# The down phase of a feed-forward block: residual tiles that stay on chip, and outputs transposed per half of the frames

## The chip, the cores and the metric

One core of a Trainium2 chip runs the whole program: one launch for one streaming step of a one-layer encoder trunk. The metric is the device time of one execution in microseconds (us), taken as the median of repeated runs. The core has five engines that take part here: TensorE (PE in the profile, with its weight loads as PEld), VectorE (DVE), ScalarE (ACT), GpSimd (POOL) and SyncE (SP). Sixteen DMA engines move data between the chip's memory (DRAM) and the on-chip tiles; SP, ACT and POOL each issue DMAs into a queue of their own, which the profile numbers q1 (SP), q10 (ACT) and q0 (POOL).

## The reference

Only the last lines of the layer matter to the change. `x` is the residual after attention and convolution; 512 prompt frames and 64 sample frames go through the same weights.

```python
    x = x + mix @ w_out
    h2 = rmsnorm(x, g_norm2)
    x = x + (jax.nn.silu(h2 @ w_gate) * (h2 @ w_up)) @ w_down
    return x, k, v, new_conv
```

Everything is float32. The model width D is 2048 (16 tiles of 128 rows, KD = 16) and the feed-forward width is 5632, which is 22 pairs of 128-row tiles (NFP = 22). The two outputs that come from the last `x` are `y_prompt` (512 x 2048) and `y_sample` (64 x 2048), with frames as rows.

## The kernel before

**Layout.** The 576 frames stand side by side (512 prompt, then 64 sample) and are cut into two halves of 288 columns (HALF, HALVES). Activations lie transposed: channels on the 128 partitions, frames along the free axis. A float32 product is made of three matmuls on a rounded part and a remainder: a weight or activation is split into a high part (a cast to fp32r) and a low part (the difference), and w_hi x_hi, w_lo x_hi and w_hi x_lo are added up in PSUM. `split` (L217 the cast on ScalarE, L218 the subtraction on VectorE) does this for weights and for activations.

**Units and products.** The feed-forward block is computed by Strassen-Winograd on 2 x 2 blocks: two output tiles of 128 channels by two halves of the frames, in seven products numbered `p_` = 1 to 7 instead of eight. One such piece of work is a unit. There are 42 gate and up units (NGU = 42) and then 36 down units, listed in `DOWN` as (d, a, b): output pair d (of eight), over the hidden pairs a to b. A down unit with m = b - a pairs has 7 products of m steps of 3 matmuls, 21m in all. The 36 units together go over each of the 8 x 22 combinations once; the last unit of each of the eight d's is among the last eight units (numbers 28 to 35 of the phase, with m = 7, 3, 7, 7, 3, 7, 5, 6), and `last` holds them.

**The order of the work.** PE's instructions run in the order in which the program gives them (the list `order`: mostly products 1, 3 and 4 of one unit interleaved with those of the next); a scheduler of the framework places those of the other engines. In `run`, products 1, 6, 5 and 3 accumulate in one PSUM tile `psy`, of which ScalarE copies out a `part` after 1, 6 and 5 (`kept`, L1076) before PE may go on adding to it; products 7 and 4 use `psw`, product 2 uses `psx`. After products 2, 5, 3 and 4 `done` hands over one block of the 2 x 2: (0,0), (1,1), (0,1) and (1,0), where the first number is the channel tile c and the second the half i.

**Weights of a down unit.** SP issues them (`load_weight`, L180), two loads per unit, into two buffers each, one unit ahead. `prepare` forms the sums and differences on VectorE (L1052 to L1056) and splits the operand of a product two products ahead (AHEAD = 2).

**The slots.** The hidden activations, in the seven forms that the products need and already split, are written to DRAM by the gate and up units (`put_form`, L923, on POOL's queue) and come back per hidden pair into one of seven tiles, the slots: 128 x 7 x 2 x 288 floats, 2016 KB each. `load_pair` (L1157 to L1160) does it with ScalarE's queue. Slots 0 to 2 take the room of the phase before, the operands h2ah, h2al and b22 of the gate and up units in `h2pool`; slots 3 to 6 lie in `dpool`, which is opened when the down phase begins. Twenty-two pairs go through seven slots, so slots are loaded again as soon as the last unit that uses them is through: `calls` lists after which unit.

**The residual.** It is `x2`, which the out projection left in DRAM (`x2_dram`), as the room on chip is taken by the gate and up units. `load_x2` (L1131 whole, L1140 in halves, POOL's queue) brings the two tiles of a unit's d, two units ahead. `add` (L1154, VectorE) adds the PSUM blocks and parts of a unit to them. `store_x2` (L1146 whole, L1150 in halves, POOL's queue) writes them back to DRAM after the unit, so that the next unit of the same d reads them again; a last unit calls `store_y` instead.

**The outputs.** `store_y` turns blocks of the finished residual on PE into PSUM (L1174; L1179 for the 64 sample frames), in groups of 1, 2 or 3 blocks of 128 frames as they become complete, copies a group into the tile `ob` (two buffers, VectorE, L1175) and stores it from POOL's queue (L1176). The sample frames go through `obs` (ScalarE, L1181) and ScalarE's queue (L1182). The work is placed by `pipe`, a list of generators that is run as the matmul steps go by; `yield 3` lets three steps pass.

Of the kernel before, what the change touches and what calls it, by code (L numbers as in the profile page):

```python
# [10 lines left out]
F32 = mybir.dt.float32  # L11
F32R = mybir.dt.float32r
# [81 lines left out]
def tile_hybrid_stream_step(  # L94
# [739 lines left out]
    h2ah = h2pool.tile([P, KD, HALF], F32R, tag="h2ah", name="h2ah")  # L834
    h2al = h2pool.tile([P, KD, HALF], F32R, tag="h2al", name="h2al")
    b22 = h2pool.tile([P, 2, NP, HALF], F32R, tag="b22", name="b22")
    b22h, b22l = b22[:, 0], b22[:, 1]
# [5 lines left out]
    def h2(kt, i):  # L843
        if i == 0:
            return h2ah[:, kt, :], h2al[:, kt, :]
        hi, lo = (b22h, b22l) if kt % 2 else (b12h, b12l)
        return hi[:, kt // 2, :], lo[:, kt // 2, :]
# [156 lines left out]
    def frames(n, p_):  # L1004

        kind, _, a, m = UNITS[n]
        if kind == "down":
            return [(slots[a + j][:, p_ - 1, 0, :], slots[a + j][:, p_ - 1, 1, :]) for j in range(m)]
        if p_ < 3:
            return [(h2ah[:, k, :], h2al[:, k, :]) for k in range(p_ - 1, KD, 2)]  # L1010
        if p_ == 3:
            return [(b22h[:, j, :], b22l[:, j, :]) for j in range(m)]
        q = {5: 0, 6: 1, 7: 2, 4: 3}[p_]
        return [(tsum[j][:, 0, q, :], tsum[j][:, 1, q, :]) for j in range(m)]
# [55 lines left out]
    def run(n, p_):  # L1070
# [8 lines left out]
        def done(c, i, ps, part=None):  # L1079
            if kind != "down":  # L1080
                return finish(kind, fp, c, i, ps, part)
            add(n, c, i, ps)
            if part is not None:
                add(n, c, i, part)
            if n in last:
                store_y(n, c, i)
            elif (c, i) == (1, 0):
                store_x2(n)
# [34 lines left out]
    first_last = min(last)  # L1123
    spare = [(tmp, "y"), (tmp, "r")], [(tmp, "sq"), (h2pool, "hx")]

    def load_x2(n):

        d, xb = UNITS[n][1], {}
        if n % 4 < 2 or n >= first_last:
            whole = down["pool"].tile([P, 2, T], F32, tag="x2", name=f"x2_{n}", bufs=2)  # L1130
            nc.gpsimd.dma_start(out=whole, in_=x2_dram[2 * d : 2 * d + 2].rearrange("k p t -> p k t"))  # L1131
            xb["whole"] = whole
        for c in range(2):
            for i, (a, b) in enumerate(HALVES):
                if "whole" in xb:
                    xb[c, i] = whole[:, c, a:b]
                    continue
                pool, tag = spare[n % 2][c]
                xb[c, i] = pool.tile([P, HALF], F32, tag=tag, name=f"x2_{n}", bufs=2)
                nc.gpsimd.dma_start(out=xb[c, i], in_=x2_dram[2 * d + c][:, a:b])  # L1140
        xt2[n] = xb

    def store_x2(n):
        d, xb = UNITS[n][1], xt2.pop(n)
        if "whole" in xb:
            nc.gpsimd.dma_start(out=x2_dram[2 * d : 2 * d + 2].rearrange("k p t -> p k t"), in_=xb["whole"])  # L1146
            return
        for c, i in ((0, 0), (1, 1), (0, 1), (1, 0)):
            a, b = HALVES[i]
            nc.gpsimd.dma_start(out=x2_dram[2 * d + c][:, a:b], in_=xb[c, i])  # L1150

    def add(n, c, i, src):
        dst = xt2[n][c, i]
        nc.vector.tensor_tensor(out=dst, in0=src, in1=dst, op=ALU.add)  # L1154

    def load_pair(p):
        tag = ("h2ah", "h2al", "b22", "s3", "s4", "s5", "s6")[p % SLOTS]  # L1157
        pool = h2pool if p % SLOTS < 3 else down["pool"]
        slots[p] = pool.tile([P, FORMS, 2, HALF], F32R, tag=tag, name=f"slot{p}")
        nc.scalar.dma_start(out=slots[p].bitcast(F32), in_=hid_dram[p])  # L1160

    def store_y(n, c, i):

        x2t, cs = xt2[n]["whole"][:, c, :], slice((2 * UNITS[n][1] + c) * P, (2 * UNITS[n][1] + c + 1) * P)
        whole = (c, 1 - i) in unit[n].setdefault("done", set())
        unit[n]["done"].add((c, i))
        b0, b1 = ((0, 2), (3, 4), (0, 3), (2, 4))[2 * whole + i]

        def work():
            yield 3  # L1170
            ob = down["pool"].tile([P, 3, P], F32, tag="ob", name="ob", bufs=2)[:, : b1 - b0]
            po = misc("pot")[:, : (b1 - b0) * P]
            for q in range(b0, b1):
                nc.tensor.transpose(po[:, (q - b0) * P : (q - b0 + 1) * P], x2t[:, q * P : (q + 1) * P], ident)  # L1174
            nc.vector.tensor_copy(out=ob, in_=po.rearrange("p (i c) -> p i c", c=P))  # L1175
            nc.gpsimd.dma_start(out=yp[b0 * P : b1 * P, cs].rearrange("(i p) c -> p i c", p=P), in_=ob)  # L1176
            if i:
                po2 = misc("pot2")
                nc.tensor.transpose(po2[:TS, :P], x2t[:, TP:], ident)  # L1179
                os_ = down["pool"].tile([TS, P], F32, tag="obs", name="obs", bufs=2)  # L1180
                nc.scalar.copy(out=os_, in_=po2[:TS, :P])  # L1181
                nc.scalar.dma_start(out=ys[:, cs], in_=os_)  # L1182
# [6 lines left out]
    for k_, (n, p_) in enumerate(order):  # L1189
# [4 lines left out]
        if (n, p_) == (NGU, 1):  # L1194
# [3 lines left out]
            load_x2(n)  # L1198
            load_pair(3)
            load_x2(n + 1)  # L1200
# [5 lines left out]
        if n == NGU - 1:  # L1206
            for p in {2: (0, 1), 3: (2,)}.get(p_, ()):
                load_pair(p)
        if n >= NGU and p_ == 4:
            if n + 2 < NU:  # L1210
                load_x2(n + 2)
# [37 lines left out]
```

## Time and profile before

| | us |
|---|---|
| runs shown | 2516.25, 2513.17, 2509.73 |
| median | 2513.17 |
| profiled execution, its own time | 2509.96 |
| span of that execution in the profile | 2508.2 |
| PE busy in the span | 2429.6 |
| VectorE / ScalarE / POOL busy | 1756.1 / 1069.1 / 311.5 |
| DMA moved in the span | 369.53 MB |
| of that from 1920 us on (the down phase) | 131.04 MB |

The span goes from the first to the last instruction that the profile shows; the execution's own time has 1.8 us more around it. The mean granted TensorE clock was 0.988. In the down phase, the stretch from 1920 us to the end, the DMA engines' time is shared by queues as follows (packets, megabytes, share of the sixteen engines' time in that stretch):

```profile
q1 hardware_dynamic: 88742, 44.87, 27.1%
q0 software_dynamic: 12576, 43.72, 22.1%
q10 hardware_dynamic: 4160, 41.81, 18.4%
```

The queue q1 carries the weights, q10 the slots (and the small sample outputs), q0 what POOL issues: the residual in both directions, the last forms and the prompt outputs. The transfers of the residual and the slots in the same stretch, with the number of issues, the kilobytes of each and the median us from issue to landing:

```profile
slot<-hid_dram ACTq DMA_DIRECT2D x20, 2016.0 KB, 11.1
...
x<-x_dram POOLq DMA_DIRECT2D x22, 576.0 KB, 4.5
...
x<-x_dram POOLq DMA_DIRECT2D x56, 144.0 KB, 4.8
x_dram<-x POOLq DMA_DIRECT2D x56, 144.0 KB, 5.2
x_dram<-x POOLq DMA_DIRECT2D x14, 576.0 KB, 3.3
```

And the instructions that use the residual and the output tile there (line, engine, operation, names, shapes, count, busy us and mean ns of one, then the idle time just before them and what ended it):

```profile
L1154 DVE TENSOR_TENSOR x<-part,x 128x288 f32<-128x288 f32 x108 | 49.2, 455 | 14.7 <-ACT part L1076 13.4
...
L1175 DVE COPY ob<-pot 128x256 f32<-128x256 f32 (+2 forms) x32 | 13.3, 421 | 6.9 <-PE pot L1174 5.3 <-DMA out_dram<-ob 1.4
```

Rows of this kind give the duration of one instruction and say how long its engine stood before it; a wait counts against the end only where PE, which carries most of the chain, stands too.

### The profile page before, as it was taken

The numbers are of one execution on the slowest core, as the hardware profiler recorded it, in microseconds if no ns is written. First come the engines' busy times: TensorE is split into PE (matmuls) and PEld (weight loads), VectorE is DVE, ScalarE is ACT, GpSimd is POOL, SyncE is SP. The second block draws the span as 40 slices with busy tenths as digits, with TensorE's granted clock in tenths as the row PEclk, the third lists the DMA queues.
The fourth block names the chain that finished last, engine by engine and source line by source line (L and its number), as shares of the span: only waits on it lengthen the run. The fifth ranks groups of instructions, "written<-read, shape, count | busy, mean of one in ns | idle before, by whom it ended". The sixth has DMA issues, their size and how long they took to land.

```text
span 2508.2 us, 44014 instructions
## 1 busy us (share of the span) xinstructions
PE 2429.6 (97%) x18121; PEld 2415.6 (96%) x18121; DVE 1756.1 (70%) x2772; ACT 1069.1 (43%) x1863; POOL 311.5 (12%) x545
## 2 busy tenths in 40 slices
PE   8999999999999999999999999999997898999898
PEld 8999999999999999999999999999997898999898
DVE  7766666353345458888888888888885776777676
ACT  6655555231122345444444444444442343433343
POOL 2111011110020120000010100100001221111121
PEclk9999999999999999999999999999999898999999
DMA  8322332222242343445444444445446767768753
GB/s 265 88 85 86 90 93 79 70 83 85 85 160 85 104 141 101 134 148 153 133 139 131 152 150 140 141 122 157 144 144 237 258 201 270 264 204 274 250 151 97
DMA packets 442690, 369.53 MB, mean 147 GB/s; under 512 B 11198, under 2 KB 413240, under 8 KB 439672
## 3 DMA queue, kind: packets, MB, share of 16 engines
q1 hardware_dynamic: 413624, 233.39, 32.1%
q0 software_dynamic: 24416, 87.38, 9.6%
q10 hardware_dynamic: 4448, 45.94, 4.7%
q8 instruction: 142, 2.33, 0.4%
q14 instruction: 60, 0.49, 0.1%
HBM read 285.85 MB, written 80.82 MB: 146 GB/s over the span
## 4 chain that ended last, share of the span: by engine, by line
PE 90%; DMA 4%; DVE 2%; issue 2%; ACT 1%; POOL 0%; SPq 0%; POOLq 0%; ACTq 0%; DVEq 0%
PE psy L1066 30%; PE pj L209 23%; PE psw L1066 15%; PE pjo L209 8%; PE psx L1066 7%; DMA raw<-in_w_down_dram 3%; PE pw L981 2%; DVE whl L218 1%; DMA hid_dram<-form 1%; PE z L547 1%; PE po L613 1%; DMA slot<-hid_dram 0%; PE os L643 0%; PE zs L573 0%; DVE x L1154 0%
## 5 line engine op out<-in xcount | busy, mean ns | idle before, releaser
L217 ACT CAST whl<-raw 128x1024 fp32r<-128x1024 f32 (+5 forms) x468 | 416.9, 897 | 281.1 <-issue 108.7
L218 DVE TENSOR_TENSOR whl<-raw,whl 128x1024 fp32r<-128x1024 f32 (+5 forms) x468 | 479.5, 1030 | 78.4 <-ACT whl L217 77.5
L209 PE MATMUL pj<-xhi,whi 128*128 128x288 f32 x1504 | 450.6, 300 | 0.6 <-ACT whi L172 0.6
L209 PE MATMUL pj<-xlo,whi 128*128 128x288 f32 x1504 | 444.6, 296 | 1.7 <-DVE xlo L343 1.7
L209 PE MATMUL pj<-xhi,wlo 128*128 128x288 f32 x1504 | 444.3, 295 | 0.3 <-DVE wlo L173 0.3
L1066 PE MATMUL psy<-slot,whl 128*128 128x288 f32 x2112 | 310.5, 303 | 55.2 <-ACT part L1076 19.5
L1066 PEld LDWEIGHTS psy<-slot,whl 128*128 128x128 f32 x2112 | 295.6, 194 | 59.5 <-ACT part L1076 20.3
L209 PEld LDWEIGHTS pj<-xlo,whi 128*128 128x128 f32 x1504 | 284.0, 189 | 2.1 <-DVE xlo L343 2.1
L209 PEld LDWEIGHTS pj<-xhi,whi 128*128 128x128 f32 x1504 | 284.3, 189 | 1.2 <-ACT whi L172 0.8
L209 PEld LDWEIGHTS pj<-xhi,wlo 128*128 128x128 f32 x1504 | 284.4, 189 | 0.9 <-DVE wlo L173 0.5
L1066 PE MATMUL psy<-tsum,whl 128*128 128x288 f32 x2016 | 281.1, 295 | 1.2 <-DVE whl L218 1.2
L1066 PE MATMUL psw<-tsum,whl 128*128 128x288 f32 x2016 | 281.0, 295 | 0.5 <-DVE ut L960 0.5
L1066 PEld LDWEIGHTS psy<-tsum,whl 128*128 128x128 f32 x2016 | 271.8, 189 | 1.5 <-DVE whl L218 1.5
L1066 PEld LDWEIGHTS psw<-tsum,whl 128*128 128x128 f32 x2016 | 271.8, 188 | 0.7 <-DVE ut L960 0.7
L172 ACT CAST whi<-raw 128x1024 fp32r<-128x1024 f32 (+1 forms) x138 | 140.0, 1031 | 232.3 <-PE pj L209 95.8
L1076 ACT COPY part<-psy 128x288 f32<-128x288 f32 x234 | 93.2, 398 | 327.5 <-PE psy L1066 325.6
L923 POOL DMA_DIRECT2D hid_dram<-form x154 | 83.6, 543 | 904.0 <-DVE form L218 759.9
L173 DVE TENSOR_TENSOR wlo<-raw,whi 128x1024 fp32r<-128x1024 f32 (+1 forms) x132 | 160.3, 1227 | 24.5 <-ACT whi L172 23.2
L1066 PE MATMUL psw<-slot,whl 128*128 128x288 f32 x1056 | 155.5, 298 | 0.0
L1066 PEld LDWEIGHTS psw<-slot,whl 128*128 128x128 f32 x1056 | 146.0, 190 | 0.2 <-DVE whl L218 0.2
L1066 PE MATMUL psy<-b,whl 128*128 128x288 f32 x1008 | 140.4, 295 | 0.5 <-ACT part L1076 0.5
L1066 PE MATMUL psx<-h2ah,whl 128*128 128x288 f32 x672 | 135.6, 297 | 2.6 <-DVE gs L960 2.6
(337 smaller groups left out, 4237.2 us busy)
## 6 DMA issues: line engine op xcount, KB each, us to landing
raw<-in_w_in_dram SPq DMA_DIRECT2D x47, 1024.0 KB, 5.4
raw<-in_w_gate_dram SPq DMA_DIRECT2D x44, 1024.0 KB, 5.6
raw<-in_w_up_dram SPq DMA_DIRECT2D x44, 1024.0 KB, 5.9
hid_dram<-form POOLq DMA_DIRECT2D x154, 288.0 KB, 2.5
slot<-hid_dram ACTq DMA_DIRECT2D x22, 2016.0 KB, 11.8
raw<-in_w_down_dram SPq DMA_DIRECT2D x30, 640.0 KB, 5.9
raw<-in_w_out_dram SPq DMA_DIRECT2D x16, 1024.0 KB, 5.2
x<-x_dram POOLq DMA_DIRECT2D x22, 576.0 KB, 4.5
```

Of the source, the lines that this page charges most:

```text
L172: nc.scalar.copy(out=hi[:, a:b], in_=raw[:, a:b])
L173: lo_eng.tensor_tensor(out=lo[:, a:b], in0=raw[:, a:b], in1=hi[:, a:b].bitcast(F32), op=ALU.subtract)
L209: mm(ps, w_[:, k, csl], x_[:, k, a:b], start=(k == 0 and n == 0), stop=(k == nk - 1 and n == 2))
L217: nc.scalar.copy(out=hi, in_=src)
L218: (lo_eng or nc.vector).tensor_tensor(out=lo, in0=src, in1=hi.bitcast(F32), op=ALU.subtract)
L547: mm(zb[i], a_[:, kk], b_[:, q0:TP], start=(n == 0), stop=False, skip_group_check=True)
L613: mm(po[:, i * P : 512], a_[:, i, :], b_[:, : 512 - i * P], stop=(i == 0 and n == 2), **kw)
L923: nc.gpsimd.dma_start(out=hid_dram[fp][:, n - 1], in_=t.bitcast(F32))
L981: mm(pss[j, i], w_[:, k, j * P : (j + 1) * P], x_, start=(kk == 0 and k == 0 and n == 0), stop=(kk == 1 and k == 7 and n == 2))
L1066: mm(ps, whl[:, w_, j, :], x_, start=(start and j == 0 and q == 0), stop=(j == len(xs_) - 1 and q == 2), skip_group_check=True)
L1076: nc.scalar.copy(out=t, in_=st["y"])
```

## The change

In the down phase the residual is loaded once per output pair d and stays on chip until it is turned and stored; `store_x2` is gone. The room for the eight pairs (sixteen tiles of 576 frames) is put together from tiles that the phase has no other use for:

- The operands of the gate and up units in `h2pool` are laid out anew: three tiles of fourteen 288-column pieces (tags s0 to s2, which become slots 0 to 2 later) and one of six (h2z). The operands that product 3 of the gate and up units reads (`late`) fill the third tile and the end of the fourth. h2z later holds the residual of d = 0 and one channel tile of d = 3.
- d = 1 and 2 and the other tile of d = 3 lie in `dpool` (tag x2, ten buffers); d = 4 and 5 in the temporaries y, r, sq and hx; d = 6 in the room of the row scale R; d = 7 in that of the split forms (hl).

All residual loads are now half tiles, four per d, still on POOL's queue, 32 in all. The slot loads move from ScalarE's queue to POOL's (`load_pair`). At the start of the down phase slot 2 and the residual of d = 0 are asked for after product 3 of the last up unit, and the residual of a later d is asked for two units ahead of its first use.

The outputs are turned per half: each block (c, i) is turned as soon as it is done, in two pieces of 128 frames and one of 32, so that a last unit has 12 transposes in place of 10. VectorE copies the two large pieces and ScalarE the small one into `ob`, which has one buffer; the stores are all on POOL's queue: two for half 0, and four for half 1, where the prompt's end (frame 512) cuts a piece in two (`put`).

```diff
--- before.py
+++ after.py
@@ -831,10 +831,14 @@
 
 
     h2pool = tc.alloc_tile_pool(name="h2pool", bufs=1, reuse_waits="tile", side="left")
-    h2ah = h2pool.tile([P, KD, HALF], F32R, tag="h2ah", name="h2ah")
-    h2al = h2pool.tile([P, KD, HALF], F32R, tag="h2al", name="h2al")
-    b22 = h2pool.tile([P, 2, NP, HALF], F32R, tag="b22", name="b22")
-    b22h, b22l = b22[:, 0], b22[:, 1]
+    SB = 2 * FORMS
+    h2t = [h2pool.tile([P, SB, HALF], F32R, tag=f"s{i}", name=f"h2_{i}") for i in range(3)]
+    h2t.append(h2pool.tile([P, 3 * KD - 3 * SB, HALF], F32R, tag="h2z", name="h2_z"))
+    places = [h2t[i][:, j, :] for i in range(3) for j in range(SB)] + [h2t[3][:, j, :] for j in range(3 * KD - 3 * SB)]
+    early, late = places[: 2 * SB] + places[3 * SB : 3 * SB + 4], places[2 * SB : 3 * SB] + places[3 * SB + 4 :]
+    h2a = [(early[2 * k], early[2 * k + 1]) for k in range(KD)]
+    b22s = [(late[2 * j], late[2 * j + 1]) for j in range(NP)]
     b12pool = tc.alloc_tile_pool(name="b12pool", bufs=1, reuse_waits="tile", side="left")
     b12h = b12pool.tile([P, NP, HALF], F32R, name="b12h")
     b12l = b12pool.tile([P, NP, HALF], F32R, name="b12l")
@@ -842,9 +846,8 @@
 
     def h2(kt, i):
         if i == 0:
-            return h2ah[:, kt, :], h2al[:, kt, :]
-        hi, lo = (b22h, b22l) if kt % 2 else (b12h, b12l)
-        return hi[:, kt // 2, :], lo[:, kt // 2, :]
+            return h2a[kt]
+        return b22s[kt // 2] if kt % 2 else (b12h[:, kt // 2, :], b12l[:, kt // 2, :])
 
     def after_b2(kt):
         for i, (a, b) in enumerate(HALVES):
@@ -1007,9 +1010,9 @@
         if kind == "down":
             return [(slots[a + j][:, p_ - 1, 0, :], slots[a + j][:, p_ - 1, 1, :]) for j in range(m)]
         if p_ < 3:
-            return [(h2ah[:, k, :], h2al[:, k, :]) for k in range(p_ - 1, KD, 2)]
+            return h2a[p_ - 1 :: 2]
         if p_ == 3:
-            return [(b22h[:, j, :], b22l[:, j, :]) for j in range(m)]
+            return b22s
         q = {5: 0, 6: 1, 7: 2, 4: 3}[p_]
         return [(tsum[j][:, 0, q, :], tsum[j][:, 1, q, :]) for j in range(m)]
 
@@ -1084,8 +1087,6 @@
                 add(n, c, i, part)
             if n in last:
                 store_y(n, c, i)
-            elif (c, i) == (1, 0):
-                store_x2(n)
 
         if p_ == 1:
             st["y"] = ps_pj.tile([P, HALF], F32, tag="pj", name="psy")
@@ -1120,66 +1121,65 @@
     xt2 = {}
     down = {}
 
-    first_last = min(last)
-    spare = [(tmp, "y"), (tmp, "r")], [(tmp, "sq"), (h2pool, "hx")]
-    def load_x2(n):
-        d, xb = UNITS[n][1], {}
-        if n % 4 < 2 or n >= first_last:
-            whole = down["pool"].tile([P, 2, T], F32, tag="x2", name=f"x2_{n}", bufs=2)
-            nc.gpsimd.dma_start(out=whole, in_=x2_dram[2 * d : 2 * d + 2].rearrange("k p t -> p k t"))
-            xb["whole"] = whole
+    def load_x2(d):
+        if d in (0, 3):
+            z = h2pool.tile([P, 6, HALF], F32, tag="h2z", name="x2_z") if d == 0 else xt2["z"]
+            xt2["z"] = z
         for c in range(2):
+            pool, tag = ((down.get("pool"), "x2"), (tmp, "r" if c else "y"), (h2pool, "hx") if c else (tmp, "sq"),
+                         (rpool, "R"), (tmp, "hl"))[max(d - 3, 0)]
+            if d == 0 or (d, c) == (3, 0):
+                q = 4 if d else 2 * c
+                two = z[:, q], z[:, q + 1]
+            elif d > 5:
+                t = pool.tile([P, 2, HALF], F32, tag=tag, name=f"x2_{d}", bufs=2)
+                two = t[:, 0], t[:, 1]
+            else:
+                two = [pool.tile([P, HALF], F32, tag=tag, name=f"x2_{d}", bufs=10 if d < 4 else 2) for _ in HALVES]
             for i, (a, b) in enumerate(HALVES):
-                if "whole" in xb:
-                    xb[c, i] = whole[:, c, a:b]
-                    continue
-                pool, tag = spare[n % 2][c]
-                xb[c, i] = pool.tile([P, HALF], F32, tag=tag, name=f"x2_{n}", bufs=2)
-                nc.gpsimd.dma_start(out=xb[c, i], in_=x2_dram[2 * d + c][:, a:b])
-        xt2[n] = xb
-    def store_x2(n):
-        d, xb = UNITS[n][1], xt2.pop(n)
-        if "whole" in xb:
-            nc.gpsimd.dma_start(out=x2_dram[2 * d : 2 * d + 2].rearrange("k p t -> p k t"), in_=xb["whole"])
-            return
-        for c, i in ((0, 0), (1, 1), (0, 1), (1, 0)):
-            a, b = HALVES[i]
-            nc.gpsimd.dma_start(out=x2_dram[2 * d + c][:, a:b], in_=xb[c, i])
+                nc.gpsimd.dma_start(out=two[i], in_=x2_dram[2 * d + c][:, a:b])
+                xt2[d, c, i] = two[i]
 
     def add(n, c, i, src):
-        dst = xt2[n][c, i]
+        dst = xt2[UNITS[n][1], c, i]
         nc.vector.tensor_tensor(out=dst, in0=src, in1=dst, op=ALU.add)
 
     def load_pair(p):
-        tag = ("h2ah", "h2al", "b22", "s3", "s4", "s5", "s6")[p % SLOTS]
+        tag = f"s{p % SLOTS}"
         pool = h2pool if p % SLOTS < 3 else down["pool"]
         slots[p] = pool.tile([P, FORMS, 2, HALF], F32R, tag=tag, name=f"slot{p}")
-        nc.scalar.dma_start(out=slots[p].bitcast(F32), in_=hid_dram[p])
+        nc.gpsimd.dma_start(out=slots[p].bitcast(F32), in_=hid_dram[p])
 
     def store_y(n, c, i):
 
-        x2t, cs = xt2[n]["whole"][:, c, :], slice((2 * UNITS[n][1] + c) * P, (2 * UNITS[n][1] + c + 1) * P)
-        whole = (c, 1 - i) in unit[n].setdefault("done", set())
-        unit[n]["done"].add((c, i))
-        b0, b1 = ((0, 2), (3, 4), (0, 3), (2, 4))[2 * whole + i]
+        kt = 2 * UNITS[n][1] + c
+        src, cs, f0 = xt2[kt // 2, c, i], slice(kt * P, (kt + 1) * P), HALVES[i][0]
+        def put(f, ap):
+            rows, n_p = ap.shape[0], max(min(TP - f, ap.shape[0]), 0)
+            if n_p:
+                nc.gpsimd.dma_start(out=yp[f : f + n_p, cs], in_=ap[:n_p])
+            if n_p < rows:
+                nc.gpsimd.dma_start(out=ys[f + n_p - TP : f + rows - TP, cs], in_=ap[n_p:])
 
         def work():
             yield 3
-            ob = down["pool"].tile([P, 3, P], F32, tag="ob", name="ob", bufs=2)[:, : b1 - b0]
-            po = misc("pot")[:, : (b1 - b0) * P]
-            for q in range(b0, b1):
-                nc.tensor.transpose(po[:, (q - b0) * P : (q - b0 + 1) * P], x2t[:, q * P : (q + 1) * P], ident)
-            nc.vector.tensor_copy(out=ob, in_=po.rearrange("p (i c) -> p i c", c=P))
-            nc.gpsimd.dma_start(out=yp[b0 * P : b1 * P, cs].rearrange("(i p) c -> p i c", p=P), in_=ob)
-            if i:
-                po2 = misc("pot2")
-                nc.tensor.transpose(po2[:TS, :P], x2t[:, TP:], ident)
-                os_ = down["pool"].tile([TS, P], F32, tag="obs", name="obs", bufs=2)
-                nc.scalar.copy(out=os_, in_=po2[:TS, :P])
-                nc.scalar.dma_start(out=ys[:, cs], in_=os_)
+            ob = down["pool"].tile([P, 3, P], F32, tag="ob", name="ob")
+            po = misc("pot")[:, : 3 * P]
+            for q in range(3):
+                w = min(P, HALF - q * P)
+                nc.tensor.transpose(po[:w, q * P : (q + 1) * P], src[:, q * P : q * P + w], ident)
+            nc.vector.tensor_copy(out=ob[:, :2], in_=po[:, : 2 * P].rearrange("p (i c) -> p i c", c=P))
+            r = HALF - 2 * P
+            nc.scalar.copy(out=ob[:r, 2], in_=po[:r, 2 * P :])
+            if i == 0:
+                nc.gpsimd.dma_start(out=yp[: 2 * P, cs].rearrange("(i p) c -> p i c", p=P), in_=ob[:, :2])
+            else:
+                put(f0, ob[:, 0])
+                put(f0 + P, ob[:, 1])
+            put(f0 + 2 * P, ob[:r, 2])
 
         pipe.spawn(work())
 
@@ -1195,9 +1195,8 @@
             tpool.release()
             ypool.release()
             down["pool"] = tc.alloc_tile_pool(name="dpool", bufs=1, reuse_waits="tile", side="right")
-            load_x2(n)
             load_pair(3)
-            load_x2(n + 1)
+            load_x2(1)
         if NGU < n < NGU + SLOTS - 3 and p_ == 1:
             load_pair(n - NGU + 3)
         if k_ + AHEAD < len(order):
@@ -1206,9 +1205,12 @@
         if n == NGU - 1:
             for p in {2: (0, 1), 3: (2,)}.get(p_, ()):
                 load_pair(p)
+            if p_ == 3:
+                load_x2(0)
         if n >= NGU and p_ == 4:
-            if n + 2 < NU:
-                load_x2(n + 2)
+            new = [d for d, _, _ in DOWN[: n - NGU + 3] if (d, 0, 0) not in xt2]
+            for d in new:
+                load_x2(d)
             for p in calls[n - NGU]:
                 load_pair(p)
     pipe.flush()
```

## The prediction

> **What bounds the kernel now.** I read the page first, its busy rows and its 40 slices, then busy time by stretch, then the timeline of each hole. Below are two rows of the slices, busy tenths over the span, and the page's chain of waits by engine.
>
> ```profile
> PE   8999999999999999999999999999997898999898
> ...
> DMA  8322332222242343445444444445446767768753
> ...
> PE 90%; DMA 4%; DVE 2%; issue 2%; ACT 1%; POOL 0%; SPq 0%; POOLq 0%; ACTq 0%; DVEq 0%
> ```
>
> PE is full up to slice 30 and holed only in the last ten, the down phase, where DMA is busiest. Busy time by stretch puts the holes:
>
> ```profile
> core 0: us, PE busy (x) PEld busy (x) DVE busy (x) ACT busy (x) POOL busy (x), PEclk, DMA share, GB/s
> 1820.00:1880.00 60.00, 60.00 (x454) 60.00 (x454) 49.93 (x67) 27.04 (x42) 4.87 (x9) 1.00 0.49 150
> ...
> 1920.00:1980.00 60.00, 34.77 (x209) 33.23 (x208) 32.48 (x67) 15.43 (x33) 15.11 (x27) 0.77 0.86 313
> 2070.00:2100.00 30.00, 18.21 (x118) 17.64 (x117) 15.44 (x30) 8.01 (x17) 5.98 (x11) 0.77 0.86 333
> 2200.00:2220.00 20.00, 15.39 (x102) 14.93 (x101) 11.18 (x16) 5.54 (x9) 3.81 (x7) 0.91 0.76 262
> 2330.00:2360.00 30.00, 20.61 (x137) 19.68 (x136) 16.78 (x27) 8.87 (x16) 2.16 (x3) 0.89 0.86 311
> 2360.00:2480.00 120.00, 116.96 (x874) 114.74 (x873) 93.75 (x153) 47.14 (x82) 22.87 (x33) 1.00 0.52 151
> ```
>
> PE is idle 25.2, 11.8, 4.6, 9.4 and 3.0 us in the last five rows, with DMA busy 76 to 86% in the first four of them, and the granted clock falls after each hole. The phase holds 3696 matmuls on slots (2112 psy, 1056 psw, 528 psx); the chain shows 45 of them in 6.00 us, 0.133 each, so 492.8 us of work, plus 80 transposes of 0.107. From the first (1924.6) to the last matmul (2501.8) it takes 577.2: some 76 us are holes and slow clock. Two views say what ends them. DMA traffic around the second hole, by queue (q10 slots, q1 weights, q0 POOL):
>
> ```profile
> q10 hardware_dynamic: 576, 8.26, 57.9%
> q1 hardware_dynamic: 4160, 2.10, 20.5%
> q0 software_dynamic: 504, 1.52, 11.8%
> ...
> raw<-in_w_down_dram SPq DMA_DIRECT2D x3, 512.0 KB, 13.2
> ```
>
> Four slot loads issued at 2065.0 to 2067.0 fill the engines to about 2091; the next unit's weights, issued at 2073.3, take 19.6 us (a median of 6.0 over the phase) and PE waits. The other two late holes are the same, beside loads of slots 15, 16 and 19 to 21. The first hole is of another kind; ScalarE's timeline:
>
> ```profile
> 1933.25 0.43 ACT L217 CAST form<-ux 128x288 fp32r<-128x288 f32 x1 [5.83 <-DMA hid_dram<-form]
> 1933.27 0.33 ACTq L1160 DMA_DIRECT2D slot<-hid_dram  x1
> 1941.81 0.43 ACT L217 CAST form<-ut 128x288 fp32r<-128x288 f32 x1 [8.13 <-DMA hid_dram<-form]
> ...
> 1944.37 0.39 ACT L1076 COPY part<-psy 128x288 f32<-128x288 f32 x1
> ```
>
> PE needs that part to go on (idle 8.1 us until 1944.8); ScalarE holds it behind a cast whose buffer is freed only when an earlier form store lands, and that store competes with a slot load.
>
> **What the change removes.** 70 stores and all but 32 of the 78 loads of x2: 28 units times 0.59 MB stored and as much reloaded, 33 of the phase's 138 MB, all on POOL's queue. No PE, DVE or ACT work goes with them.
>
> *Late holes.* q0 took 11.8% of 16 engines over 35 us (2060 to 2095), 4.1 us; 16.6% of 35 us (2180 to 2215), 5.8 us; 15.4% of 40 us (2325 to 2365), 6.2 us. A burst that fills the engines ends that much earlier, and PE with it, at most by the hole: 4 + 4 + 6 = **14 us**. Below: 5, if the freed time goes to slots rather than weights. Above: 26, the three holes and 0.8 at 2151, if the weights come through at once.
>
> *Start.* Slot loads move from ScalarE's queue to POOL's, behind the form stores there. Slot 2, which PE waits for, is issued after the (1,1) form store as now (1924.6) and may land as late (8.9 us): no gain. But in the new instruction order the part follows the third cast, which needs only the store ahead of it on the same queue, done soon after slot 2 (about 1934): PE goes on near 1935.5 instead of 1944.8. Slot 3 is issued after three more forms and four x2 loads (0.55 us each), near 1937 instead of 1933.3, and lands near 1946; unit 1, which ran its first product at 1951, gains 5 there. The weights of unit 2 are issued 10 us earlier than 1952.2, land 16.5 later as now, and PE reaches unit 2 at 1960 instead of 1971.3; the next weights, now issued among slots 5 and 6, give 2 or 3 back. **9 us**; from 2 (every slot as late as slot 3) to 19 (of PE's 27 us lateness at 1971 only the wait for slot 2 stays). If POOL stands, what queues behind it is only x2 loads and later slots.
>
> *Order on VectorE.* In seven units the add of psw (L1154) stands ahead of the split of s (L218), and PE waits 1.15 us for it (2265.0 to 2266.3, for one). In the new instruction order this occurs in none. Three of the seven lie beside a late hole; 4 times 1.15: **4.6 us**, from 0 to 5.7.
>
> **What it adds.** *Transposes*: 96 instead of 80, 16 times 0.107 = **1.7 us** on PE.
>
> *The output buffer.* This is the part that can spoil it. ob has one buffer instead of two, each of 32 halves uses it, and each copy into it waits on VectorE, in order, for the stores of the half before. All stores are POOL's, 96 instead of 32 (16 of ScalarE's go). Now they land so, all 32 first, then by size (KB each, median us):
>
> ```profile
> DMA to landing us min/median/max: 2.0/3.2/6.5
> ```
> ```profile
> out_dram<-ob POOLq DMA_DIRECT2D x16, 128.0 KB, 2.3
> out_dram<-ob POOLq DMA_DIRECT2D x8, 192.0 KB, 3.6
> ...
> out_dram<-ob POOLq DMA_DIRECT2D x8, 64.0 KB, 4.1
> ```
>
> One turn of the buffer: copy 0.42, 0.41 to POOL's issue (2490.55 to 2490.96), then the issues before the last (0.75 in the first half; 0.58 and twice about 0.55 in the second, small ones priced as the smallest seen), then a landing of 2.0: 3.6 and 4.5 us, 16.2 for the four of a unit. A unit of seven pairs runs 147 times 0.133 = 19.6 us, six 16.8, five 14.0, three 8.4. So the buffer keeps up except in the two units of three (short by 7.8 each) and the one of five (2.2). Behind a late copy stand weight splits two products ahead and one more turned half in the second PSUM bank, about one turn of 4: left over 4 + 4, and nothing at the five. Where weights are loading, stores now take 3.8 to 6.5; once a unit, 2.7 us more than 2.2, against a slack of 3.4: 3 in all. **11 us.** Below 0 (all absorbed); above 33: every turn at the median landing of 3.2 is 4.8 and 5.7, 168 us for 32, against 134.3 from the first turned block (2369.1) to the last (2503.4).
>
> *End.* The last copy waits for the stores of the half before (4.5 against 2.55 between the copies), 2.0, and then for a second issue, 0.75, less 0.5 for a shorter landing: **2.3 us**.
>
> **Sum.** 14 + 9 + 4.6 - 1.7 - 11 - 2.3 = 12.6 us less. The profiled execution took 2509.96 (span 2508.2), so **2497**. The median, 2513.17, is 3.2 above that execution, inside the spread of the three; the price is the same from either.
>
> **A rule of the skill.** The Trainium skill, "DMA: Bandwidth & Descriptors", section "Queues, rings and completion order", says that each engine turns between queues packet by packet. Its section "SWDGE vs HWDGE vs iDMA" gives a packet of GpSimd's as preferably at most 4096 B. In this trace q10's packets average 10.3 KB and q0's 3.6; by the rule, slots on POOL's queue would let weights through sooner. The page's specifications speak the other way, with a first byte 0.4 us later from GpSimd; no row here isolates that.
>
> **Rivals.**
> *Weights come through.* Now weights end with the slot burst, though they are a tenth of its bytes. If loads from POOL's queue share better with q1 than those from ScalarE's, the late holes give 22 of 26, the start 13: 22 + 13 + 4.6 - 15 = 24.6 less, **2485**. For it: weights beside q0 alone take 6.8 us (2360 to 2508). Against: nothing here shows slots on q0.
> *The traffic was hidden.* The x2 transfers ran in the gaps and slots alone set the holes: 5 + 2 + 4.6 against 15, **2513**. For it: q0 is the smallest of the three shares. Against: the engines are full to 2091.
> *The buffer becomes the bound* (slower). Place: the eight last units; price 33 for 11; it decides once landings average over about 2.6, since the turns then outlast even the long units. 2510 - 27.6 + 37 = 2519, and 2528 if the gains are at 60%: **2522**. For it: the median of 3.2 now, small stores slowest (4.1). Against: of the 32, the 12 with neither an x2 load nor weights beside them took 2.0 to 2.3, and x2 loads are gone.
> That it does not do what it says is ruled out: the built order has 32 x2 transfers after the spill, no store.
>
> **Chances.** Forecast 0.46, weights through 0.17, hidden 0.14, buffer 0.23. About 0.3% (7.5 us) is what a measurement can tell here. Faster: nearly all of the first two and little else, 0.58; within: 0.17; slower: most of the buffer case and a little of the hidden one, 0.25. Bounds of all terms together give 2464 to 2543; eight in ten lie in 2474 to 2524. The forecast's own range is 2486 to 2507.
>
> **What would show it.** Right: no x2 stores; PE reaching its second unit of four pairs near 1960; each late hole shorter; no wait of PE on a split of s; VectorE's ob copies waiting for out stores, a few us per short unit. Wrong: holes of unchanged length beside slots (hidden), weights at 6 us beside slots (through), or VectorE waiting for out stores by 1 us or more in nearly every half and the stretch from first turned block to end above 155 us against 139 (buffer).

## The result, and the profile after

The changed kernel takes 2518.82 us in the median of 9 runs (2514.56 to 2520.80), the kernel before 2511.64 in the median of 9 (2509.73 to 2516.25). The ratio is 1.0024, with a 95% interval of 1.0014 to 1.0034: slower by some 6 us (the means are 6.1 apart, the medians 7.2), clear of noise though below the 0.3% named in the prediction. The forecast was 2497 with a range of its own of 2486 to 2507: the time lies above that range, inside the 2474 to 2524 given for eight cases in ten, and the change went the other way. The profiled execution of the changed kernel took 2514.56 us, the shortest of the nine; its span is 2512.9, 4.7 above the span before.

The rows of the page that answer those shown of before, first the slices and then the chain:

```profile
PE   8999999999999999999999999999998798999887
...
DMA  8322332222242343444444544434446635656532
...
PE 87%; DMA 5%; DVE 3%; issue 2%; POOL 1%; ACT 1%; SPq 0%; POOLq 0%; DVEq 0%; ACTq 0%
```

DMA is less busy in the last ten slices, and yet PE is lower at the very end, where it was at 8 and 9 before. The down phase by queue, in the stretch from 1920 us on, and what POOL issued there (KB each, median us to landing):

```profile
q1 hardware_dynamic: 89590, 45.30, 27.3%
q0 software_dynamic: 8145, 52.31, 23.9%
...
slot<-hid_dram POOLq DMA_DIRECT2D x20, 2016.0 KB, 9.8
...
x<-x_dram POOLq DMA_DIRECT2D x24, 144.0 KB, 6.8
...
out_dram<-ob POOLq DMA_DIRECT2D x48, 16.0 KB, 1.7
```

No store of the residual is left, and its traffic and the slots now share q0: 52.3 MB, where q0 and q10 together had 85.5. So the change does what it says. Busy time by stretch (columns as in the prediction):

```profile
1920.00:1980.00 60.00, 33.76 (x203) 33.06 (x202) 27.93 (x58) 14.35 (x31) 22.06 (x41) 0.74 0.92 326
2070.00:2100.00 30.00, 19.18 (x129) 18.70 (x128) 15.05 (x30) 8.41 (x17) 0.89 (x2) 0.83 0.79 309
2200.00:2220.00 20.00, 20.00 (x154) 20.00 (x153) 18.65 (x25) 9.24 (x13) 0.00 (x0) 1.00 0.51 171
2330.00:2360.00 30.00, 22.89 (x161) 22.41 (x160) 18.26 (x28) 9.79 (x15) 1.25 (x2) 0.89 0.37 127
2360.00:2480.00 120.00, 104.65 (x781) 101.26 (x780) 81.98 (x135) 43.39 (x86) 39.57 (x71) 1.00 0.38 105
```

The first stretch has 26.2 us of idle PE (25.2 before), the three late ones 10.8, 0 and 7.1 (11.8, 4.6 and 9.4), and the output stretch 15.4 (3.0). PE runs the same matmuls in the same order in all the kernels here but for the transposes, so they can be counted off by unit. The next table was made so from the traces: us from the first matmul on a slot to the end of unit 8 ("start"), from there to the end of unit 27 ("late holes"), from there to the end of unit 35 ("outputs"), and from the last matmul to the end of the span.

| profile | first matmul | start | late holes | outputs | end | span |
|---|---|---|---|---|---|---|
| before | 1924.6 | 142.3 | 297.5 | 137.4 | 6.4 | 2508.2 |
| changed | 1926.4 | 143.8 | 278.7 | 153.4 | 10.5 | 2512.9 |
| difference | +1.8 | +1.5 | -18.8 | +16.0 | +4.1 | +4.7 |
| predicted | 0 | -9 | -18.6 | +12.7 | +2.3 | -12.6 |

The first matmul lies between 1923.4 and 1932.7 in the twelve profiles of this study; 1.8 us there are within what it varies by. What stands out is the start, which gained nothing, and the outputs, which cost more than forecast.

### The profile page after: what moved, and what is told of

It is laid out like the page before. It is cut to its first block, busy times and chain, and to the rows that moved or that the text cites. A ratio compares the mean times of both kernels' runs of the same rounds, so it can differ in the third digit from the quotient of the medians.

```text
span 2512.9 us, 44035 instructions
## 1 busy us (share of the span) xinstructions
PE 2427.3 (97%) x18137; PEld 2414.1 (96%) x18137; DVE 1759.8 (70%) x2772; ACT 1073.3 (43%) x1879; POOL 284.8 (11%) x515
## 3 DMA queue, kind: packets, MB, share of 16 engines
q0 software_dynamic: 20352, 100.29, 10.5%
## 4 chain that ended last, share of the span: by engine, by line
PE 87%; DMA 5%; DVE 3%; issue 2%; POOL 1%; ACT 1%; SPq 0%; POOLq 0%; DVEq 0%; ACTq 0%
PE psy L1069 29%; PE pj L209 23%; PE psw L1069 14%; PE pjo L209 8%; PE psx L1069 7%; DMA raw<-in_w_down_dram 3%; PE pw L984 2%; DMA out_dram<-ob 2%; POOL out_dram L1163 1%; DVE xlo L343 1%; PE z L547 1%; DVE whl L218 1%; PE po L613 1%; DMA hid_dram<-form 0%; POOL out_dram L1165 0%
## 5 line engine op out<-in xcount | busy, mean ns | idle before, releaser
L217 ACT CAST whl<-raw 128x1024 fp32r<-128x1024 f32 (+5 forms) x468 | 419.2, 897 | 278.7 <-issue 111.3
L1069 PE MATMUL psy<-slot,whl 128*128 128x288 f32 x2112 | 305.4, 301 | 44.3 <-DVE whl L218 21.4
L1069 PE MATMUL psy<-h,whl 128*128 128x288 f32 x1764 | 248.8, 296 | 0.5 <-ACT part L1079 0.5
L1069 PEld LDWEIGHTS psy<-h,whl 128*128 128x128 f32 x1764 | 239.8, 189 | 0.7 <-ACT part L1079 0.7
```

The lines of the kernel that those rows point to most:

```text
L217: nc.scalar.copy(out=hi, in_=src)
L1069: mm(ps, whl[:, w_, j, :], x_, start=(start and j == 0 and q == 0), stop=(j == len(xs_) - 1 and q == 2), skip_group_check=True)
```

## The experiments

Each is an edit of the changed kernel (names with a_) or of the kernel before (b_). Medians stand beside the ratio to before on the same chip. The stages of all of them, as in the table above:

| kernel | start | late holes | outputs | end | median | ratio to before (95%) |
|---|---|---|---|---|---|---|
| changed, again (after_2) | 142.6 | 278.9 | 154.0 | 10.6 | 2518.11 | 1.0029 (1.0017 to 1.0041) |
| a_ob2 | 141.3 | 279.1 | 140.1 | 7.0 | 2498.53 | 0.9944 (0.9932 to 0.9957) |
| a_x2sp | 139.2 | 280.5 | 154.7 | 10.1 | 2514.28 | 1.0010 (1.0001 to 1.0018) |
| a_slotact | 150.2 | 285.2 | 154.4 | 9.9 | 2532.68 | 1.0074 (1.0061 to 1.0086) |
| b_slotpool | 129.9 | 308.1 | 140.4 | 6.3 | 2512.95 | 1.0000 (0.9991 to 1.0009) |
| b_half2 | 143.5 | 298.8 | 140.9 | 6.5 | 2517.64 | 1.0018 (1.0009 to 1.0027) |
| b_half1 | 143.4 | 298.8 | 155.2 | 10.2 | 2533.12 | 1.0082 (1.0068 to 1.0096) |
| a_ob2_slotact_pace | 146.3 | 286.8 | 140.4 | 6.4 | 2506.86 | 0.9980 (0.9972 to 0.9989) |
| a_ob2_pace_s1 | 139.6 | 279.4 | 139.8 | 6.5 | 2495.67 | 0.9939 (0.9927 to 0.9952) |
| a_ob2_pace | 134.9 | 281.7 | 139.8 | 6.5 | 2488.74 | 0.9909 (0.9892 to 0.9926) |

**The changed kernel again (after_2).** No edit.

> The changed kernel once more, for a second profile. If the late weights of unit 2 and the buffer's turns are what happens in every execution, PE ends unit 2 again between 1990 and 1995 us, with a weight load of more than 25 us before it, and the way from the end of unit 28 to the end of unit 35 is again 132 to 136 us; if the start is a matter of luck, unit 2 ends more than 4 us elsewhere.

The same picture, within all the bounds expected: PE ends unit 2 at 1993.5 behind a weight load of 29.8 us, the way from the end of unit 28 to the end of unit 35 is 134.5, and PE's one long wait at the start is 15.8 us. The two profiles differ by 1.4 us in span.

**Two output buffers (a_ob2).** With a second `ob` the pool `dpool` would take 77.25 KB per partition, and 77 are left for it. So the large and the small pieces have tiles of their own, two of each, one of the small ones in the room of a tile (`cst`) that is dead by then.

```diff
-            ob = down["pool"].tile([P, 3, P], F32, tag="ob", name="ob")
+            ob = down["pool"].tile([P, 2, P], F32, tag="ob", name="ob", bufs=2)
+            turns[0] += 1
+            os_ = (rpool.tile([32, P], F32, name="cst") if turns[0] % 2 else
+                   down["pool"].tile([32, P], F32, tag="os", name="os"))
```

> The changed kernel with two buffers for the turned blocks instead of one. In the changed kernel's profile the eight last units lose 15.7 us against before (from 15.2 ahead at the end of unit 28 to 0.5 behind at the end of unit 35) and the end 4.1 us more. Single buffer: if the one buffer makes the loss, PE ends unit 35 at least 11 us earlier than in the changed kernel measured from unit 28, the end shrinks by 3 or 4, and the time is 12 to 17 us below the changed kernel (ratio to before near 0.997). Rival, the 96 stores on POOL and the three pieces per half make it: the loss stays within 4 us of 15.7 and the ratio stays at 1.001 to 1.003.

The time falls by 20 us against the changed kernel's 2518.82, more than the 12 to 17 expected (the spans of the two profiles differ by 16.1; that of the changed kernel is from its shortest run, that of a_ob2 from its median one), and is below before by 0.56%. In the outputs 13.3 us come back, at the end 3.5; start and late holes stay. What VectorE waited for in the output part, us in total, times and longest, first in the changed kernel, then with two buffers:

```profile
DVE ob L1174 <- DMA out_dram<-ob: 30.2, 15, 3.9
```
```profile
DVE ob L1178 <- DMA out_dram<-ob: 1.4, 1, 1.4
```

The 96 stores are the same in both; it is the one buffer that made VectorE wait for them. At the end of the span the same can be seen in VectorE's timeline of the changed kernel, whose last copy waits for the stores of the half before:

```profile
2503.32 0.42 DVE L1174 COPY ob<-pot 128x256 f32<-128x256 f32 x1
2507.57 0.42 DVE L1174 COPY ob<-pot 128x256 f32<-128x256 f32 x1 [3.83 <-DMA out_dram<-ob]
```

**Outputs turned per half, in the kernel before (b_half1, b_half2).** `store_y` of the changed kernel put into the kernel before, with one buffer and with two.

```diff
-        x2t, cs = xt2[n]["whole"][:, c, :], ...
+        src, cs, f0 = xt2[n][c, i], slice(kt * P, (kt + 1) * P), HALVES[i][0]
...
-            ob = down["pool"].tile([P, 3, P], F32, tag="ob", name="ob", bufs=2)[:, : b1 - b0]
+            ob = down["pool"].tile([P, 3, P], F32, tag="ob", name="ob")
```

> The kernel before with the outputs turned per half and stored in 96 pieces from POOL's queue, but with two buffers. If the buffer alone made the loss of the output part, the way from the end of unit 28 to the end of unit 35 is 119 to 122 us (before 118.1, changed 133.8) and the time is 1 to 6 us above before. If the turns per half and the stores make it, 127 us or more.

> The kernel before with the outputs turned per half, with one buffer as in the change. Buffer theory: 10 to 16 us longer than the same with two buffers, the loss in the units of three pairs and behind them (units 29 to 33), none in the units of seven without one before them. Rival: within 4 us of the same with two buffers.

With two buffers the way from unit 28 to unit 35 takes 121.4 us against 118.1 before, with one 135.7. So the buffer's price, 14.3 there and 3.7 at the end, is the same away from everything else that the change does, and the turns per half with their stores cost 3.3 alone. Of the 14.3, 13.8 have come by the end of unit 33, in the units that were named.

**The slots back on ScalarE's queue (a_slotact), and onto POOL's in the kernel before (b_slotpool).**

```diff
-        nc.gpsimd.dma_start(out=slots[p].bitcast(F32), in_=hid_dram[p])
+        nc.scalar.dma_start(out=slots[p].bitcast(F32), in_=hid_dram[p])
```

> The changed kernel with the slots back on ScalarE's queue. Traffic theory of the three late holes (18.7 us gained between the ends of units 8 and 27): the gain stays, 14 or more. Queue theory (slots share better with weights on POOL's queue): most of it goes, 6 or less stay. At the start: the flood of residual loads stays, so by the flood theory PE ends unit 2 at 1988 us or later; by the theory that POOL's queue holds the weights up, at 1985 or earlier.

> The kernel before with the slots on POOL's queue and nothing else changed. Traffic theory of the late holes: the holes stay, PE's way from the end of unit 8 to the end of unit 27 is within 5 us of before's 297.5. Queue theory: it is 12 to 19 us shorter. At the start POOL's residual loads and stores now stand between the slots: PE ends unit 2 between 1985 and 1995 us.

Neither theory of the late holes held whole. Without the move of the queue 12.3 of the 18.8 us stay (14 or more were expected by the one theory, 6 or less by the other); the rest goes in four steps of some 1.5 us, at the ends of units 15, 21, 24 and 26, which the changed kernel and b_slotpool both gain and a_slotact does not. These are the units in which before a split waited behind an addition on VectorE. PE's wait for such splits between units 8 and 27 in the kernel before (us in total, times, longest), and with only the queue moved:

```profile
PE psy L1066 <- DVE whl L218: 15.6, 9, 4.1
```
```profile
PE psy L1066 <- DVE whl L218: 1.1, 3, 0.4
```

So the better order on VectorE comes with the slots' queue, not with the residual; a_slotact still has 11.1 us of such waits. In b_slotpool the late holes are longer than before all the same, by 10.6: there the slots stand on POOL's queue behind loads that wait for the residual's stores (the half-tile loads alone waited 73.3 us for those in that stretch).

At the start the theory that POOL's queue as such holds the weights up falls: b_slotpool has the slots on it, and its start is 12.4 us shorter than before, with unit 2 ended at 1980.5, below the 1985 to 1995 expected. In a_slotact the start is 6.4 us longer still than in the changed kernel, but for another reason than there: its later load of unit 2's weights took 17.8 us and not 29.2, and was asked for only at 1962.6. On ScalarE's queue the slot loads again run against the form stores, and ScalarE waits 27.7 us for those in place of 8.3:

```profile
ACT form L217 <- DMA hid_dram<-form: 27.7, 4, 11.9
```

**The residual on SP's queue (a_x2sp).**

```diff
-                nc.gpsimd.dma_start(out=two[i], in_=x2_dram[2 * d + c][:, a:b])
+                nc.sync.dma_start(out=two[i], in_=x2_dram[2 * d + c][:, a:b])
```

> The changed kernel with the 32 residual loads on SP's queue, where they queue behind the weights, instead of POOL's. Flood: if the start is late because 26 residual loads go out beside the slots between 1942 and 1974 us and unit 2's second weight load takes 29.2 us in that burst, that load lands within 17 us, PE ends unit 2 at 1985 us or earlier (before 1988.9, changed 1992.2), and the time falls by 6 to 12 us. Rival, the slots on POOL's queue alone hold the weights up: unit 2 ends within 3 us of 1992.2 and the time stays within 3 us.

Of little use as a test of the flood: 25 residual loads stand on SP ahead of unit 2's weights, which went out only at 1964.09 instead of 1942. PE ended unit 2 at 1988.7, 3.5 earlier than in the change, which is neither of the two outcomes expected. But one piece of the chain says more than the total; it is one of unit 2's two weight loads, issued when slot 6 had landed (1963.4), with nothing but other loads of SP's queue beside it:

```profile
1964.09 4.37 DMA raw<-in_w_down_dram
```

**The residual held until it is near its use (a_ob2_pace), with slots 4 to 6 behind it; the same with the slots on ScalarE's queue (a_ob2_slotact_pace), and with slots 4 to 6 sent first (a_ob2_pace_s1).** All have two output buffers.

```diff
+                if after is not None:
+                    nc.vector.tensor_copy(out=two[i][:, :1], in_=after[:, :1])
                 nc.gpsimd.dma_start(out=two[i], in_=x2_dram[2 * d + c][:, a:b])
...
-                load_x2(d)
+                load_x2(d, xt2[UNITS[n][1], 1, 0])
```
```diff
-            load_pair(3)
+            for p in range(3, SLOTS):
+                load_pair(p)
             load_x2(1)
-        if NGU < n < NGU + SLOTS - 3 and p_ == 1:
-            load_pair(n - NGU + 3)
```

> The changed kernel with two output buffers, and each residual load of d = 2 to 7 held until the unit two ahead of it has been added up (VectorE first copies one column into the tile); slots 4 to 6 stand behind these loads on POOL's queue and are held with them. Burst theory: unit 2's second weight load lands when the burst of slots 4 to 6 and 26 residual loads ends, not a fixed time after its issue; with the burst spread out it lands within 15 us of its issue, PE ends unit 2 at 1984 us or earlier (1993.3 with two buffers alone), and the time falls by 6 to 12 us from 2498.5. Rival, the weights are late whatever stands beside them (the new layout of the operands, the order of VectorE): unit 2 ends within 3 us of 1993.3.

> The same with the slots back on ScalarE's queue, so that only the residual loads are held and slots 4 to 6 are free. With the slots on ScalarE's queue and the residual free, PE ended unit 2 at 2000.4 us and the time was 2532.7, of which the one buffer makes some 16. If the early residual loads are what lengthens the start, unit 2 ends at 1992 us or earlier and the time is 2503 to 2509; if the slots alone are, it ends at 1997 or later and the time is 2513 to 2518.

> As with two output buffers and the residual loads held (2488.7 us, PE ends unit 2 at 1981.9), but slots 4 to 6 asked for together with slot 3, so that they go out back to back ahead of the residual loads and nothing holds them. If slots alone, sent ahead of need, hold up the weights of unit 2, PE ends unit 2 at 1988 us or later and the time is 2494 to 2500; if it takes the residual loads beside them, it ends within 3 us of 1981.9 and the time stays at 2487 to 2491.

Held, the start shrinks by 6.4 us against a_ob2 (2.6 are lost again in the late holes), PE ends unit 2 at 1981.9, and the kernel takes 2488.74 us, the fastest here, 0.91% below before. With slots 4 to 6 sent ahead and only the residual held, unit 2 ends at 1994.3 and the time is 2495.67, both as expected if the slots alone hold the weights up. The 1994.3 says less than it seems to, as this profile's first matmul, at 1932.7, is the latest of the twelve. Counted from the first matmul, unit 2 ends after 64.0 us in a_ob2, 61.6 with the residual held and the slots ahead of it, and 56.9 with the slots held too: most of the gain comes with the slots, about a third with the residual. With the slots on ScalarE's queue unit 2 ended at 1995.3, between the two bounds expected, so that run does not part the two; its time, 2506.86, fell into the range of the residual's share. The weight load of unit 2 that the chain runs through, in the changed kernel, in a_ob2_pace_s1 and in a_ob2_pace (start and length in us):

```profile
1942.56 29.16 DMA raw<-in_w_down_dram
```
```profile
1945.65 23.36 DMA raw<-in_w_down_dram
```
```profile
1939.33 15.96 DMA raw<-in_w_down_dram
```

In a_ob2_pace it is one microsecond over the 15 that were expected. From 4.4 to 29.2 us for the same bytes: it is what stands beside the load that sets its time. In a_ob2_pace it landed 0.8 us after slot 4, in the changed kernel 0.7 after slot 6.

## Why the prediction was wrong

**The start: the step that failed.** The prediction said that unit 2's weights are issued 10 us earlier and "land 16.5 later as now". Everything up to there came as written. ScalarE's timeline of the changed kernel has the part right behind the third cast, at 1936.0 (forecast near 1935.5):

```profile
1935.63 0.43 ACT L217 CAST form<-ut 128x288 fp32r<-128x288 f32 x1 [7.92 <-DMA hid_dram<-form]
1936.00 0.40 ACT L1079 COPY part<-psy 128x288 f32<-128x288 f32 x1
```

Slot 3 went out at 1937.6 and landed at 1947.1 (forecast 1937 and 1946), the weights went out at 1941.7 and 1942.6 (forecast 1942), and PE was free for unit 2 at 1958.6. There it stopped: it ran one matmul of it and stood for 14.6 us. It went on at 1973.5, where 1960 was forecast and 1971.3 is the time before. First the piece of the chain before, then the chain of the changed kernel:

```profile
1952.71 17.14 DMA raw<-in_w_down_dram
```
```profile
1942.56 29.16 DMA raw<-in_w_down_dram
...
1971.81 0.06 DVE s L1055
...
1972.87 0.61 DVE whl L218
...
1973.52 5.89 PE psy L1069 x23
```

A landing of 16.5 us was read from one burst and carried to another as if it were the load's own. It was the time that was left of the burst: before, the weights were asked for at 1952 and came at 1968 and 1970, with slots 5 and 6 about; in the changed kernel they were asked for at 1942 and came at 1972, because slots 4, 5 and 6, which no unit uses before unit 4 (1998.5), and 20 residual loads, most of them for later units, all went out between 1942 and 1972. The queue rows of the changed kernel show what moved in those 30 us (packets, MB, share), first from 1942 to 1952, then from 1952 to 1972:

```profile
q0 software_dynamic: 455, 2.58, 71.3%
q1 hardware_dynamic: 1949, 0.98, 33.3%
```
```profile
q0 software_dynamic: 1067, 7.92, 98.7%
q1 hardware_dynamic: 131, 0.06, 1.1%
```

The weights are a tenth of the bytes, and most of them were not late: 1949 of the 2080 packets had moved by 1952, when the first of unit 2's two loads landed, 9.8 us after its issue. The last 131 took the other 20 us, and a load is there only when its last packet is. By the Trainium skill, "DMA: Bandwidth & Descriptors", section "Queues, rings and completion order", each engine takes a packet from each queue in turn. Where both queues have much to move, the rows agree with it. First the kernel before, from 1954 to 1964, slots on q10; then a_ob2_pace_s1, from 1952 to 1966, slots on q0:

```profile
q10 hardware_dynamic: 240, 3.42, 84.5%
...
q1 hardware_dynamic: 213, 0.11, 3.7%
```
```profile
q0 software_dynamic: 403, 5.81, 97.1%
q1 hardware_dynamic: 401, 0.20, 4.8%
```

One packet of weights moved for about one packet of a slot, and it holds some 500 B where the slot's holds some 14 KB, so the weights crawl until the slots are through. In the changed kernel after 1952 it was one for eight. By the same rule only a few of the sixteen engines would then still have had weights to move; the rows are by queue and not by engine, so that is not shown. The prediction used the rule the other way round, from q0's mean packet of 3.6 KB. That mean was of residual and outputs; a slot load is 144 packets of 14.3 KB on average on either queue (8.26 MB in 576 for four of them in both kernels). So the move to POOL's queue changed nothing in that, and the 4096 B that the prediction quoted for a packet of GpSimd's is not what the slot loads show.

The residual's traffic was thus not only removed. What is left of it was no longer paced by stores and reused buffers, so it went out as soon as POOL could issue it, into the one burst in which PE was waiting for weights, on the same queue as the slots: slot 6 landed at 1971.0, where it was 1965.9 before. a_ob2_pace, which holds it and the slots, gains 6.4 us in the start against a_ob2 and 7.4 against before, of the 9 predicted.

**The late holes: right in mechanism and sum, with some luck in the parts.** 18.6 forecast, 18.8 measured; 12.3 with the traffic alone gone (forecast 14) and the rest with VectorE's order (forecast 4.6; the four steps make some 6). That the order comes from the slots' queue was not seen. By hole the traffic was to give 4, 4 and 6; at the ends of units 10, 18 and 27 the changed kernel gained 1.4, 6.8 and 2.3. The hole at 2200 is gone (PE 20.0 of 20), the one at 2070 is the least changed (10.8 for 11.8): there slots 7 to 10 meet the weights as before.

**The output buffer: mechanism right, size too small.** The turns of the buffer were forecast at 3.6 us for half 0 and 4.5 for half 1. Of half 1 the last two of the changed kernel took 4.5 and 4.3; one of half 0, which ended with a wait for its stores, took 4.2 (from 2380.4 to 2384.5). 31 turns fill the 153.0 us from the first copy to the last, 4.9 each. The mean counts idle time in the long units. The term was 11 and 2.3 at the end; a_ob2 gives 13.3 and 3.5 as the price of the one buffer. The step that was off is "left over 4 + 4": the weight splits and one more turned half in PSUM were to take up half of the 7.8 us by which a unit of three is short. Against a_ob2, the changed kernel loses 4.9 us over units 29 to 31, behind the first unit of three, and 7.5 over 32 and 33, behind the second: there nearly the whole of the 7.8.

**The turns per half** cost 2.7 us (a_ob2) to 3.5 (b_half2) in the outputs against 1.7 forecast from 16 transposes. What the other 1 or 2 us are was not traced.

**The rivals.** "Weights come through" falls: at the start the load took 29.2 us beside slots on POOL's queue, and in the hole at 2070 a load still took 19.7 beside four slots (19.6 before). "The traffic was hidden" falls: the late holes lost 12 us with it. "The buffer becomes the bound" has its place right, and VectorE waits at 15 of 32 copies; but it was to cost 33 in the units and to outlast the long ones too, and it costs 13.3. Of its two signs one came, 159 us from the first turned block to the end (155 were named), and not the other, a wait in nearly every half. Its time, 2522, lies 3 us above the median for another reason: the start did not pay. (Two of the prediction's sums come out otherwise, without changing the forecast: at 60% of the gains 2510 - 16.6 + 37 is 2530, not 2528, and the upper bound of all terms, from the 2510 of the sum, is 2540, not 2543.)

Summed up against the forecast of -12.6: of the 17.3 us between -12.6 and +4.7 the start makes 10.5, the buffer with its end 3.5, the turns per half 1.6, and the first matmul, which varies by more than that from profile to profile, 1.8. The medians differ by 2.6 us more than the two profiled executions do.

## What to carry to other kernels

A landing time that was read in a burst is not the transfer's: ask when the burst ends, and what joins it when a wait that spread the loads out is taken away. Loads that are ready early should be held until near their use if a load that is needed now shares the engines with them. And a tile that a copy fills and a store empties needs two buffers as soon as its turn (copy, issue, landing: 4.2 to 4.5 us here) is longer than the work that fills it; a quarter of a kilobyte of room decided here between 0.24% slower and 0.56% faster.

## What was not expected of the hardware

A 512 KB weight load of unit 2 took 4.4, 16.0, 23.4 and 29.2 us in four kernels, beside slot loads in all but the first of these. In the slowest case it was not the bulk that was late: 94% of the packets of unit 2's two loads had moved by 1952, some 10 us after their issue, and for the last 6% PE stood still for 14.6 us. And putting slots on the queue of an engine that also waits for stores moved 12 us from one stage to another at no gain: b_slotpool is 12.4 us shorter at the start, 10.6 longer in the late holes and 3.0 longer in the outputs than before, with a ratio of 1.0000.
